# One 1/rms per token tile for the keys of eight heads, and the factor of the query parts moved into the squares

## The chip, the core and the metric

The kernel runs on one core of a Trainium2 chip. The core has engines that each work through their own queue in order: TensorE (PE in the profile, with its weight loads as PEld) for matrix products, VectorE (DVE), ScalarE (ACT) and GpSimd (POOL) for work on elements, SyncE (SP) for starting transfers. Results of TensorE land in a small memory, PSUM, from which ACT or DVE copy them. The metric is the device time of one execution in microseconds; the lower the better.

## The reference

One step of a two-layer streaming encoder. 576 tokens are worked: 512 of a prompt and 64 of a sample that has 512 tokens of past in caches. Every layer adds to x the output projection of three mixers, which share one input projection (stick-breaking attention, gated linear attention, latent attention), then a cross attention into 256 memory tokens, then a gated feed-forward part. The change touches the latent attention alone:

```python
def rmsnorm(x, g):
    y = xf * lax.rsqrt(jnp.mean(xf * xf, axis=-1, keepdims=True) + NORM_EPS)
    return (y * g).astype(x.dtype)

q = (rmsnorm(cq, w['g_cq']) @ w['w_uq']).reshape(B, T, 8, 64 + 32)
q_nope = rmsnorm(q[..., :64], w['g_qn'])
q_rope = rope(rmsnorm(q[..., 64:], w['g_qr']), q_pos)
kv = (lat_all @ w['w_ukv']).reshape(B, L, 8, 64 + 64)
k_nope = rmsnorm(kv[..., :64], w['g_kn'])
v = kv[..., 64:]
s = (q_nope . k_nope + q_rope . k_rope) * 96 ** -0.5        # then a softmax over the visible keys, times v
```

So each head's query has a part of 64 columns and one of 32, each with its own root mean square (rms), and each head's key has 64 columns with one. The keys' rms is taken per token and head.

## The kernel before, in words

Tokens lie in tiles of 128 rows, the last one of 64 (the sample). Products that need near-f32 precision are made of three matmuls: an operand is split into a rounded high part H and a rest L (`copyA` to H on ACT, a subtraction to L on DVE; for weights these are the tiles `wH` and `wL`), and H·H, H·L and L·H are added in PSUM (`mm3`). PSUM has eight banks with three tags: D three, S two, T three.

The order of the work is planned while the program is built. The class `Order` holds the mixers as generators that yield where a result has to come back from another engine, and takes at each step the task of lowest rank that is ready by the class `Clock`, which books each instruction on its engine with an estimated cost. Output-projection products (phase `wout`) and input products have a rank of 10: they fill PE while a task of rank 0 waits. Each engine's queue then has one fixed order, and an instruction waits there for its semaphores, with all that stands behind it.

The two functions of the change:

- `mlaq_units.unit` (lines 1185 to 1218), ten units per layer: two halves `a` of four heads, five token tiles `t`. Six matmuls into an S bank; ACT copies it to `j` (`q3`) and squares it into `u` (`sq`); DVE multiplies the 32-column parts by the gain, POOL by the sine table; DVE sums the squares of both parts of four heads into the eight columns of `s`, line 1208 halves the first four (a mean over 64 from a scaling by 1/32), and `rstd_near` makes 1/rms of all eight at once. POOL multiplies both parts by it (lines 1212 and 1213), PE transposes the four heads into a T bank, ACT copies that into `qT`. The transposes wait for POOL.
- `kv_tile` (lines 1388 to 1415), nine tiles per layer: four of the prompt, four of the past, one of the sample. In a loop over two halves of four heads: three matmuls into an S bank, POOL copies the rotary key in, ACT copies the key part into `j` (`k`), squares it into `kp` (`sq`), copies the values; DVE sums the squares into four columns, `rstd_near` makes 1/rms of the four, DVE multiplies the keys. After the loop PE transposes both halves.

`rstd_near` (lines 386 to 396) is six instructions whatever the width: a tensor_scalar on DVE, Ln and Exp on ACT, and one Newton step of a product and two scalar_tensor_tensor on DVE, in the tiles `s` and `y`. All these lines call helpers, so the profile shows one line, L195, for all of them; instructions are told apart by the tiles' names. `mlaq0` is the phase of the queries in layer 0, `mlak0` that of the keys, `mlap0` the attention of the prompt, `wout0` the output projection, `sb0` the stick-breaking attention.

Of the kernel before, what the change touches and what calls it, by code (L numbers as in the profile page):

```python
# [13 lines left out]
AF = mybir.ActivationFunctionType  # L14
ALU = mybir.AluOpType
AX = mybir.AxisListType
# [162 lines left out]
def behind(tc, ins, earlier):  # L179
    tc.add_manual_dep(ins, earlier.name, mybir.DependencyInfo(mybir.DependencyClass.NoSync, mybir.DependencyReason.DATA),  # L180
                      reason="order of an engine")
# [35 lines left out]
def tile_hybrid(ctx, tc, ins, outs):  # L217
    clock = tc.clock = Clock()
    nc = Engines(tc)
# [16 lines left out]
    def nm(s):  # L236
        uid[0] += 1
        return f"{phase[0]}.{s}_{uid[0]}"
# [26 lines left out]
    def small(n, tag="s"):  # L265
        bufs = {"s": 8, "y": 4}.get(tag, 1)
        return clock.tile(sp.tile([128, 16 if tag == "y" else 8], F32, tag=tag, name=nm(tag), bufs=bufs), tag, bufs)[:, :n]
# [15 lines left out]
    def act(out, in_, func, **kw):  # L283
        name = TABLES.get(func)
        if name is not None and name != held["set"]:
            load = nc.scalar.preload_act_table_set(name).ins
            for i in held["users"]:
                behind(tc, load, i)
            held.update(set=name, load=load, users=[load])
        ins = nc.scalar.activation(out, in_, func, **kw).ins  # L290
        if name is not None:
            behind(tc, ins, held["load"])
            held["users"].append(ins)
# [7 lines left out]
    def tt(out, a, b, op, eng=None):  # L301
        (eng or nc.vector).tensor_tensor(out, a, b, op=op)
# [4 lines left out]
    MUL, ADD, SUB = ALU.mult, ALU.add, ALU.subtract  # L307
# [78 lines left out]
    def rstd_near(ss, inv_n):  # L386

        rows, n = ss.shape[0], ss.shape[1]
        y = small(2 * n, "y")[0:rows]
        y0, z = y[:, 0:n], y[:, n:2 * n]  # L390
        nc.vector.tensor_scalar(ss, ss, inv_n, EPS, op0=MUL, op1=ADD)
        act(z, ss, AF.Ln)
        act(y0, z, AF.Exp, scale=-0.5)
        tt(z, y0, y0, MUL)
        stt(z, z, -0.5, ss, MUL, MUL)
        stt(ss, z, 1.5, y0, ADD, MUL)
# [501 lines left out]
    def layer(l, xn):  # L898
# [283 lines left out]
        def mlaq_units():  # L1182
            hold = {}

            def unit(a, t, r0, rn):
                if a not in hold:
                    hold[a] = load_w(I["w_uq"][l, :, a * 384:(a + 1) * 384], 2, 384, by="k")
                w, cT = hold[a], st["cT"]
                d = ps_("S")[0:rn, 0:384]
                for k in range(2):  # L1190
                    mm3(d, cT[:, k, r0:r0 + rn], cT[:, 2 + k, r0:r0 + rn], w[0](k, 0, 384), w[1](k, 0, 384), k == 0, k == 1)
                if a and t == 4:
                    od.event("mlaqw")
                s = small(8)[0:rn]
                q3 = u("j")[0:rn, 0:384]
                copyA(q3, d)
                sq = u()[0:rn, 0:384]
                act(sq, q3, AF.Square)
                s3, q3 = (x.rearrange("p (h c) -> p h c", c=96) for x in (sq, q3))
                qf = q3[:, :, 64:96]  # L1200
                tt(qf, qf, gbl[0:rn, 160:192].unsqueeze(1).broadcast_to([rn, 4, 32]), MUL)
                qs = small4()[0:rn].rearrange("p (h c) -> p h c", c=32)
                q4, qs4 = (x.rearrange("p h (b c) -> p h b c", c=16) for x in (qf, qs))
                tt(qs4, q4[:, :, ::-1, :], rS[0:rn, t, :].rearrange("p (b c) -> p b c", c=16).unsqueeze(1).broadcast_to(
                    [rn, 4, 2, 16]), MUL, nc.gpsimd)
                nc.vector.tensor_reduce(s[:, 0:4], s3[:, :, 0:64], axis=AX.X, op=ADD)
                nc.vector.tensor_reduce(s[:, 4:8], s3[:, :, 64:96], axis=AX.X, op=ADD)
                nc.vector.tensor_scalar(s[:, 0:4], s[:, 0:4], 0.5, None, op0=MUL)
                tt(q4, q4, rC[0:rn, t, :].unsqueeze(1).unsqueeze(1).broadcast_to([rn, 4, 2, 16]), MUL)
                tt(qf, qf, qs, ADD)  # L1210
                rstd_near(s, 1.0 / 32)
                tt(q3[:, :, 0:64], q3[:, :, 0:64], s[:, 0:4].unsqueeze(2).broadcast_to([rn, 4, 64]), MUL, nc.gpsimd)
                tt(qf, qf, s[:, 4:8].unsqueeze(2).broadcast_to([rn, 4, 32]), MUL, nc.gpsimd)
                yield "T"
                pt = ps_("T").rearrange("p (h c) -> p h c", c=128)
                for h in range(4):
                    tr(pt[0:96, h, 0:rn], q3[:, h, :])
                copyA(qT[a][0:96, :, r0:r0 + rn], pt[0:96, :, 0:rn], scale=gT[0:96, 78 + l:79 + l])

            for a in range(2):  # L1220
                for t, (r0, rn) in enumerate(TILES):
                    yield [f"cT{t}", "sb", "rg"], unit(a, t, r0, rn), None
# [165 lines left out]
        def kv_tile(c0, rn, kr, kT, kc, vdst):  # L1388
            if wkv[0] is None:
                wkv[0] = load_w(I["w_ukv"][l], 1, 1024, by="k")  # L1390
            w, lat = wkv[0], st["lat"]
            ks = []
            vdst = vdst()
            for a in range(2):
                d = ps_("S")[0:rn]
                mm3(d, lat[:, 0, c0:c0 + rn], lat[:, 1, c0:c0 + rn],
                    w[0](0, a * 512, (a + 1) * 512), w[1](0, a * 512, (a + 1) * 512), True, True)
                d3 = d.rearrange("p (h c) -> p h c", c=128)
                k = u("j")[0:rn, 0:384].rearrange("p (h c) -> p h c", c=96)
                sq = u("kp")[0:rn, 0:256].rearrange("p (h c) -> p h c", c=64)  # L1400
                nc.gpsimd.tensor_copy(k[:, :, 64:96], kr().unsqueeze(1).broadcast_to([rn, 4, 32]))
                copyA(k[:, :, 0:64], d3[:, :, 0:64])
                act(sq, k[:, :, 0:64], AF.Square)
                copyA(vdst[a].rearrange("p (h c) -> p h c", c=64), d3[:, :, 64:128])
                q = small(4)[0:rn]
                nc.vector.tensor_reduce(q, sq, axis=AX.X, op=ADD)
                rstd_near(q, 1.0 / 64)
                tt(k[:, :, 0:64], k[:, :, 0:64], q.unsqueeze(2).broadcast_to([rn, 4, 64]), MUL)
                ks.append(k)
            yield "T"  # L1410
            for a in range(2):
                pt = ps_("T").rearrange("p (h c) -> p h c", c=128)
                for h in range(4):
                    tr(pt[0:96, h, 0:rn], ks[a][:, h, :])
                copyA(kT()[a][0:96, :, kc:kc + rn], pt[0:96, :, 0:rn])
# [357 lines left out]
```

## Time and profile before

| what | before |
|---|---|
| median of three timed runs | 1716.88 us (1714.28 to 1719.4) |
| the profiled execution | 1715.26 us |
| its span, first to last instruction | 1713.5 us |
| PE busy | 1649.6 us (96%) |
| DVE busy | 1230.8 us (72%) |
| ACT busy | 903.9 us (53%) |
| POOL busy | 206.8 us (12%) |
| mean granted TensorE clock | 0.99 |

The profile is of one execution; the busy times are shares of its span. Matmuls overlap in TensorE, so two neighbours' durations may cover the same time. Layer 0 runs to some 850 us, layer 1 after it. The queries of the latent attention are made between about 215 and 254 us in layer 0, the key tiles between 249 and 306 us, and the same work of layer 1 lies some 845 us later. Where a wait is told, the engine stood still and the named instruction of the other engine was the last that it waited for.

### The profile page before, as it was taken

Reading aid. Unit: us, or ns where it says so; the run is one execution under the profiler, and the core shown is the slowest. Engines: PE = TensorE matmul, PEld = TensorE weight load, DVE = VectorE, ACT = ScalarE, POOL = GpSimd, SP = SyncE. Lnnn points to the kernel's source line nnn. Section 1 sums busy time; section 2 is a strip of 40 time slices with the busy share of each in tenths; the row PEclk is TensorE's granted clock in tenths of the full one; section 3 lists DMA queues with packets and bytes.
Section 4 is the critical chain, followed back from the end, with each engine's and each line's share of the span. In section 5 each row is a group of like instructions: output and inputs, shape, how many; then the busy total and the mean of one; then the engine's idle time right before and its main releaser. Section 6 shows DMA issues by size and latency. Waiting matters only on the chain.

```text
span 1713.5 us, 30864 instructions
## 1 busy us (share of the span) xinstructions
PE 1649.6 (96%) x12231; PEld 1532.3 (89%) x12231; DVE 1230.8 (72%) x2496; ACT 903.9 (53%) x1929; POOL 206.8 (12%) x303
## 2 busy tenths in 40 slices
PE   8999999999899999999999989999998999999998
PEld 7887887789889999999998978877897999999998
DVE  5737798776898677766657378987669986766763
ACT  6426688655654444344343456886666544334431
POOL 4323341020000000000134042400200000000000
PEclk9999999999999999999998999999999999999999
DMA  5321130022022322222222213200211233233221
GB/s 165 112 72 58 64 116 26 26 74 75 25 80 93 99 80 93 99 85 89 79 83 84 81 47 98 82 26 25 99 50 50 75 99 99 74 99 99 77 97 56
DMA packets 113647, 133.30 MB, mean 78 GB/s; under 512 B 10610, under 2 KB 95712, under 8 KB 113504
## 3 DMA queue, kind: packets, MB, share of 16 engines
q1 hardware_dynamic: 113120, 131.30, 24.2%
q8 instruction: 96, 1.57, 0.4%
q14 instruction: 47, 0.39, 0.1%
q0 software_dynamic: 352, 0.03, 0.0%
q10 hardware_dynamic: 32, 0.01, 0.0%
HBM read 123.64 MB, written 7.68 MB: 77 GB/s over the span
## 4 chain that ended last, share of the span: by engine, by line
PE 76%; DVE 13%; ACT 4%; issue 3%; POOL 2%; DMA 0%; POOLq 0%; ACTq 0%; DVEq 0%
PE ffn1.D L195 9%; PE ffn0.D L195 9%; PE ffn1.S L195 6%; PE ffn1.T L195 6%; PE ffn0.S L195 6%; PE ffn0.T L195 6%; PE win1.D L195 5%; PE win0.D L195 4%; PE cross0.D L195 3%; PE cross1.D L195 3%; PE wout1.D L195 2%; PE wout0.D L195 2%; PE cross0.T L195 1%; PE cross1.T L195 1%; PE mlap1.T L195 1%
## 5 line engine op out<-in xcount | busy, mean ns | idle before, releaser
L195 ACT ACTIVATE ffn1.wH<-ffn1.wraw 128x1024 fp32r<-128x1024 f32 x66 | 60.6, 918 | 115.8 <-PE ffn1.T L195 61.5
L195 ACT ACTIVATE ffn0.wH<-ffn0.wraw 128x1024 fp32r<-128x1024 f32 x66 | 60.6, 918 | 110.5 <-PE ffn0.T L195 60.0
L195 DVE TENSOR_TENSOR ffn1.sL<-ffn1.sum,ffn1.sH 128x1024 fp32r<-128x1024 f32 x44 | 53.7, 1221 | 40.3 <-ACT ffn1.sH L195 40.3
L195 DVE TENSOR_TENSOR ffn0.sL<-ffn0.sum,ffn0.sH 128x1024 fp32r<-128x1024 f32 x44 | 53.7, 1221 | 39.9 <-ACT ffn0.sH L195 39.8
L195 PE MATMUL ffn0.D<-cross0.bT,ffn0.sH 128*128 128x288 f32 x352 | 72.4, 297 | 2.4 <-ACT ffn0.sH L195 1.5
L195 PE MATMUL ffn1.D<-cross1.bT,ffn1.sH 128*128 128x288 f32 x352 | 73.1, 299 | 1.5 <-ACT ffn1.sH L195 0.9
L195 DVE TENSOR_TENSOR ffn0.wL<-ffn0.wraw,ffn0.wH 128x1024 fp32r<-128x1024 f32 x66 | 68.8, 1043 | 7.8 <-ACT ffn0.wH L195 7.2
L195 DVE TENSOR_TENSOR ffn1.wL<-ffn1.wraw,ffn1.wH 128x1024 fp32r<-128x1024 f32 x66 | 68.8, 1043 | 7.8 <-ACT ffn1.wH L195 7.3
L195 PE MATMUL ffn1.S<-cross1.bT,ffn1.sH 128*128 128x288 f32 x352 | 72.6, 297 | 1.0 <-ACT cross1.bT L195 0.5
L195 PE MATMUL ffn0.S<-cross0.bT,ffn0.sH 128*128 128x288 f32 x352 | 71.9, 294 | 0.8 <-ACT cross0.bT L195 0.5
L195 POOL TENSOR_TENSOR ffn0.u<-ffn0.u,ffn0.u 128x576 f32<-128x576 f32 x6 | 10.0, 1664 | 469.5 <-DVE ffn0.wL L195 462.5
L195 ACT ACTIVATE ffn1.sH<-ffn1.sum 128x1024 fp32r<-128x1024 f32 x44 | 46.3, 1055 | 27.1 <-PE ffn1.S L195 22.9
L195 PEld LDWEIGHTS ffn0.D<-cross0.bT,ffn0.sH 128*128 128x128 f32 x352 | 56.7, 189 | 4.0 <-ACT ffn0.sH L195 1.9
L195 ACT ACTIVATE ffn0.sH<-ffn0.sum 128x1024 fp32r<-128x1024 f32 x44 | 46.3, 1055 | 26.0 <-PE ffn0.S L195 22.8
L195 PEld LDWEIGHTS ffn1.D<-cross1.bT,ffn1.sH 128*128 128x128 f32 x352 | 57.3, 191 | 2.9 <-ACT ffn1.sH L195 1.3
L195 PEld LDWEIGHTS ffn1.S<-cross1.bT,ffn1.sH 128*128 128x128 f32 x352 | 57.6, 191 | 1.7 <-ACT cross1.bT L195 0.8
L195 PEld LDWEIGHTS ffn0.S<-cross0.bT,ffn0.sH 128*128 128x128 f32 x352 | 57.0, 189 | 1.4 <-ACT cross0.bT L195 0.8
L195 PE MATMUL ffn1.D<-cross1.bT,ffn1.sL 128*128 128x288 f32 x176 | 52.6, 299 | 0.0
L195 PE MATMUL ffn1.S<-cross1.bT,ffn1.sL 128*128 128x288 f32 x176 | 52.5, 299 | 0.0
L195 PE MATMUL ffn0.D<-cross0.bT,ffn0.sL 128*128 128x288 f32 x176 | 52.4, 298 | 0.0
L195 PE MATMUL ffn0.S<-cross0.bT,ffn0.sL 128*128 128x288 f32 x176 | 52.2, 297 | 0.0
L195 ACT ACTIVATE ffn0.part<-ffn0.D 128x288 f32<-128x288 f32 x66 | 26.9, 408 | 41.7 <-PE ffn0.D L195 41.7
(875 smaller groups left out, 6458.6 us busy)
## 6 DMA issues: line engine op xcount, KB each, us to landing
ffn0.wraw<-in_w_gate_dram SPq DMA_DIRECT2D x11, 1024.0 KB, 5.3
ffn0.wraw<-in_w_up_dram SPq DMA_DIRECT2D x11, 1024.0 KB, 5.5
ffn0.wraw<-in_w_down_dram SPq DMA_DIRECT2D x11, 1024.0 KB, 5.0
ffn1.wraw<-in_w_gate_dram SPq DMA_DIRECT2D x11, 1024.0 KB, 5.3
ffn1.wraw<-in_w_up_dram SPq DMA_DIRECT2D x11, 1024.0 KB, 5.4
ffn1.wraw<-in_w_down_dram SPq DMA_DIRECT2D x11, 1024.0 KB, 5.0
win1.wraw<-in_w_in_dram SPq DMA_DIRECT2D x7, 1024.0 KB, 5.3
win0.wraw<-in_w_in_dram SPq DMA_DIRECT2D x6, 1024.0 KB, 5.7
```

What stands on the lines that cost most here:

```text
L195: r = fn(*args, **kw)
```

## The change

In `kv_tile` the sums of squares of both halves go into one tile of eight columns, `rstd_near` runs once for it after the loop, and the two multiplications of the keys stand behind it. In `mlaq_units.unit` the square is made by two activations, one for the 64-column parts with an input scale of 0.5 ** 0.5 and one for the 32-column parts; the halving of the four sums goes.

```diff
@@ mlaq_units.unit
                 sq = u()[0:rn, 0:384]
-                act(sq, q3, AF.Square)
                 s3, q3 = (x.rearrange("p (h c) -> p h c", c=96) for x in (sq, q3))
+                act(s3[:, :, 0:64], q3[:, :, 0:64], AF.Square, scale=0.5 ** 0.5)
+                act(s3[:, :, 64:96], q3[:, :, 64:96], AF.Square)
...
                 nc.vector.tensor_reduce(s[:, 0:4], s3[:, :, 0:64], axis=AX.X, op=ADD)
                 nc.vector.tensor_reduce(s[:, 4:8], s3[:, :, 64:96], axis=AX.X, op=ADD)
-                nc.vector.tensor_scalar(s[:, 0:4], s[:, 0:4], 0.5, None, op0=MUL)
@@ kv_tile
             vdst = vdst()
+            ss = small(8)[0:rn]
             for a in range(2):
...
                 copyA(vdst[a].rearrange("p (h c) -> p h c", c=64), d3[:, :, 64:128])
-                q = small(4)[0:rn]
-                nc.vector.tensor_reduce(q, sq, axis=AX.X, op=ADD)
-                rstd_near(q, 1.0 / 64)
-                tt(k[:, :, 0:64], k[:, :, 0:64], q.unsqueeze(2).broadcast_to([rn, 4, 64]), MUL)
+                nc.vector.tensor_reduce(ss[:, 4 * a:4 * a + 4], sq, axis=AX.X, op=ADD)
                 ks.append(k)
+            rstd_near(ss, 1.0 / 64)
+            for a, k in enumerate(ks):
+                tt(k[:, :, 0:64], k[:, :, 0:64], ss[:, 4 * a:4 * a + 4].unsqueeze(2).broadcast_to([rn, 4, 64]), MUL)
             yield "T"
```

Since the planner books the instructions as they are made, the order changes on PE, DVE, ACT and POOL through both layers' mixer stages; SP's queue keeps its order, and so do all engines in the other stages. Three places follow.

The first is PE in layer 0, behind the two sums of the stick-breaking norm (`sb0.T`), where the first query unit's product (`j_2523`) is to be transposed. Before, the output projection comes next:

```order
L195 MATMUL mlaq0.S_2606<-mlaq0.wH_2511,win0.cT_1821 128x384
L195 MATMUL sb0.T_2636<-sb0.u_2573,bd_111 128x288
L195 MATMUL sb0.T_2639<-sb0.u_2573,bd_111 128x288
L195 MATMUL wout0.D_2656<-wout0.wH_2648,wout0.mH_1505 128x256
L195 MATMUL wout0.D_2656<-wout0.wL_2649,wout0.mH_1505 128x256
```

After, the transpose and the next unit's product come first:

```order
L195 MATMUL mlaq0.S_2606<-mlaq0.wH_2511,win0.cT_1821 128x384
L195 MATMUL sb0.T_2636<-sb0.u_2573,bd_111 128x288
L195 MATMUL sb0.T_2639<-sb0.u_2573,bd_111 128x288
L195 MATMUL mlaq0.T_2646<-ident,mlaq0.j_2523 96x128 x4
L195 MATMUL mlaq0.S_2652<-mlaq0.wH_2511,win0.cT_1821 128x384
```

The 24 matmuls of that output block stood ahead of the transpose and now stand behind it and behind the six of the next unit.

The second is DVE at the same place: the Newton step of the first unit (`y_2535`, `s_2522`) and the two weight splits of the output projection. Before:

```order
L195 COPY wout0.mkv_2195<-wout0.D_2579 128x256
L195 TENSOR_TENSOR mlaq0.y_2535<-mlaq0.y_2535 128x8
L195 TENSOR_TENSOR wout0.wL_2649<-wout0.wraw_2646,wout0.wH_2648 128x1024
L195 SCALAR_TENSOR_TENSOR mlaq0.y_2535<-mlaq0.y_2535,mlaq0.s_2522 128x8
L195 TENSOR_TENSOR mlaq0.y_2564<-mlaq0.y_2564 128x8
L195 TENSOR_TENSOR wout0.wL_2653<-wout0.wraw_2646,wout0.wH_2652 128x1024
L195 SCALAR_TENSOR_TENSOR mlaq0.s_2522<-mlaq0.y_2535 128x8
```

After:

```order
L195 TENSOR_TENSOR mlaq0.y_2535<-mlaq0.y_2535 128x8
L195 TENSOR_TENSOR mlaq0.j_2552<-mlaq0.j_2552,rC 128x4x32
L195 SCALAR_TENSOR_TENSOR mlaq0.y_2535<-mlaq0.y_2535,mlaq0.s_2522 128x8
L195 TENSOR_SCALAR mlaq0.s_2551<-mlaq0.s_2551 128x8
L195 TENSOR_TENSOR mlaq0.j_2552<-mlaq0.j_2552,mlaq0.s_378_2558 128x4x32
L195 SCALAR_TENSOR_TENSOR mlaq0.s_2522<-mlaq0.y_2535 128x8
L195 COPY wout0.mkv_2195<-wout0.D_2579 128x256
L195 TENSOR_TENSOR wout0.wL_2684<-wout0.wraw_2681,wout0.wH_2683 128x1024
```

Both scalar_tensor_tensor of the first unit have moved ahead of both weight splits; small instructions of the second unit (`j_2552`, `s_2551`) stand between them instead.

The third is DVE at the first key tile of layer 0. Before, each half has its own series (`s_3072`, `y_3074` for the first, `s_3092`, `y_3094` for the second):

```order
L195 TENSOR_REDUCE mlak0.s_3092<-mlak0.kp_3087 128x4
L195 TENSOR_SCALAR mlak0.s_3092<-mlak0.s_3092 128x4
L195 TENSOR_TENSOR mlak0.y_3074<-mlak0.y_3074 128x4
L195 SCALAR_TENSOR_TENSOR mlak0.y_3074<-mlak0.y_3074,mlak0.s_3072 128x4
L195 SCALAR_TENSOR_TENSOR mlak0.s_3072<-mlak0.y_3074 128x4
L195 TENSOR_TENSOR X<-X,wout0.D_3142 128x288
L195 TENSOR_TENSOR mlak0.j_3066<-mlak0.j_3066,mlak0.s_3072 128x4x64
L195 TENSOR_TENSOR mlak0.y_3094<-mlak0.y_3094 128x4
```

After:

```order
L195 TENSOR_REDUCE mlak0.s_3018<-mlak0.kp_3024 128x4
L195 TENSOR_REDUCE mlak0.s_3018<-mlak0.kp_3035 128x4
L195 TENSOR_SCALAR mlak0.s_3018<-mlak0.s_3018 128x8
L195 TENSOR_REDUCE mlak0.s_3050<-mlak0.kp_3056 128x4
L195 TENSOR_TENSOR mlak0.y_3041<-mlak0.y_3041 128x8
L195 SCALAR_TENSOR_TENSOR mlak0.y_3041<-mlak0.y_3041,mlak0.s_3018 128x8
L195 SCALAR_TENSOR_TENSOR mlak0.s_3018<-mlak0.y_3041 128x8
L195 TENSOR_TENSOR mlak0.j_3023<-mlak0.j_3023,mlak0.s_3018 128x4x64
L195 TENSOR_TENSOR mlak0.j_3034<-mlak0.j_3034,mlak0.s_3018 128x4x64
```

One series of eight columns has taken the place of two of four, and the multiplications of both halves (`j_3023`, `j_3034`) follow one another.

## Rows read from the trace of the kernel before

**Rows 1.** The page: busy time by engine, and the chain's shares by engine.
```profile
PE 1649.6 (96%) x12231; PEld 1532.3 (89%) x12231; DVE 1230.8 (72%) x2496; ACT 903.9 (53%) x1929; POOL 206.8 (12%) x303
...
PE 76%; DVE 13%; ACT 4%; issue 3%; POOL 2%; DMA 0%; POOLq 0%; ACTq 0%; DVEq 0%
```

**Rows 2.** Windows: length, busy PE, PEld, DVE, ACT, POOL, clock, DMA.
```profile
225.00:260.00 35.00, 31.01 (x204) 26.77 (x203) 32.61 (x126) 28.13 (x79) 16.17 (x31) 1.00 0.32 109
...
260.00:300.00 40.00, 39.77 (x275) 32.11 (x273) 33.33 (x131) 33.91 (x124) 3.78 (x11) 1.00 0.09 27
...
300.00:340.00 40.00, 39.95 (x273) 27.31 (x272) 31.87 (x87) 27.41 (x66) 0.00 (x0) 1.00 0.09 27
...
1070.00:1105.00 35.00, 31.01 (x205) 26.77 (x204) 32.60 (x124) 27.94 (x78) 16.36 (x32) 1.00 0.32 111
...
245.00:260.00 15.00, 13.94 (x89) 11.65 (x89) 13.77 (x53) 12.82 (x42) 5.64 (x13) 1.00 0.22 71
```

**Rows 3.** Waits of PE, 215 to 265 and 1060 to 1110: total, times, longest.
```profile
PE mlaq0.T L195 <- POOL mlaq0.j L195: 3.6, 6, 1.5
PE mlak0.T L195 <- DVE mlak0.y L195: 0.3, 1, 0.3
...
PE mlaq1.T L195 <- POOL mlaq1.j L195: 3.6, 6, 1.5
```

**Rows 4.** The chain that ended last, 214 to 262: start, us, what.
```profile
218.78 0.60 DVE mlaq0.s L195 x3
...
220.31 1.14 DVE wout0.wL L195
221.60 1.14 DVE wout0.wL L195
...
238.65 1.13 DVE mlaq0.s L195 x4
```

**Rows 5.** Instructions by tile, layer 0: ns min/median/max, first and last start, forms.
```profile
L195 DVE TENSOR_SCALAR mlaq0.s<-mlaq0.s x20: 148/160/603, 218.0 to 248.8; 128x4 f32<-128x4 f32 x8, 128x8 f32<-128x8 f32 x8, 64x4 f32<-64x4 f32 x2, 64x8 f32<-64x8 f32 x2
...
L195 ACT ACTIVATE mlaq0.u<-mlaq0.j x10: 507/520/527, 216.0 to 246.3; 128x384 f32<-128x384 f32 x8, 64x384 f32<-64x384 f32 x2
...
L195 ACT ACTIVATE mlak0.kp<-mlak0.j x18: 399/412/435, 250.9 to 300.5; 128x256 f32<-128x256 f32 x16, 64x256 f32<-64x256 f32 x2
...
L195 DVE TENSOR_SCALAR mlak0.s<-mlak0.s x18: 151/170/414, 252.0 to 301.4; 128x4 f32<-128x4 f32 x16, 64x4 f32<-64x4 f32 x2
...
L195 ACT ACTIVATE mlak0.y<-mlak0.y x18: 187/198/220, 252.7 to 302.7; 128x4 f32<-128x4 f32 x16, 64x4 f32<-64x4 f32 x2
...
L195 DVE SCALAR_TENSOR_TENSOR mlak0.y<-mlak0.y,mlak0.s x18: 144/156/249, 253.2 to 303.2; 128x4 f32<-128x4 f32 x16, 64x4 f32<-64x4 f32 x2
```

**Rows 6.** DVE in order of time: start us, us, operation, tiles.
```profile
217.96 0.16 DVE L195 TENSOR_SCALAR mlaq0.s<-mlaq0.s 128x4 f32<-128x4 f32 x1
218.03 0.28 DVE L195 TENSOR_TENSOR mlaq0.j<-mlaq0.j,rC 128x128 f32<-128x128 f32 x1
...
220.15 0.16 DVE L195 TENSOR_TENSOR mlaq0.y<-mlaq0.y 128x8 f32<-128x8 f32 x1
...
239.18 0.60 DVE L195 TENSOR_SCALAR mlaq0.s<-mlaq0.s 128x4 f32<-128x4 f32 x1
239.70 0.28 DVE L195 TENSOR_TENSOR mlaq0.j<-mlaq0.j,rC 128x128 f32<-128x128 f32 x1
```

**Rows 7.** ACT in order of time: the squares of the first key tile.
```profile
250.87 0.41 ACT L195 ACTIVATE mlak0.kp<-mlak0.j 128x256 f32<-128x256 f32 x1
...
251.70 0.41 ACT L195 ACTIVATE mlak0.kp<-mlak0.j 128x256 f32<-128x256 f32 x1
```

**Rows 8.** PE and POOL in order of time; in brackets the idle time before.
```profile
221.15 0.49 PE L195 MATMUL wout0.D<-wout0.wH,wout0.mH 128*128 128x256 f32 x1
...
228.95 0.64 PE L195 MATMUL mlaq0.T<-ident,mlaq0.j 128*96 128x128 f32 x4 [1.46 <-POOL mlaq0.j L195]
...
222.89 1.05 POOL L195 TENSOR_TENSOR mlaq0.j<-mlaq0.j,mlaq0.s 128x256 f32<-128x256 f32 x2 [3.77 <-DVE mlaq0.y L195]
```

## The prediction

> **What bounds the kernel now.** I read the page first, then the windows around the two places that the change touches, then who waits for whom, the chain of waits, and last the instructions in order of time. The page [rows 1] shows TensorE (PE) busy in 1649.6 of 1713.5 us and the chain that ended last at 76% on PE and 13% on VectorE (DVE): whatever moves the time has to close PE's gaps, 63.9 us in all, since no matmul is added or removed. Most gaps lie elsewhere: the windows of layer 0 [rows 2] show 3.99 us of idle PE between 225 and 260 us, where the queries of the latent attention are made, but only 0.23 us in the next 40 us and 0.05 us in the 40 after that, where most of the key tiles are worked. Layer 1 repeats this to a hundredth of a microsecond (31.01 of 35.00). The waits [rows 3] name the gaps: 3.6 us per layer, in six pieces, is a query transpose that waits for its POOL multiplication, and 0.3 us, once, a key transpose that waits for DVE.
>
> Behind POOL stands DVE. In 225 to 260 DVE is busy 32.61 of 35.00 us, ScalarE (ACT) 28.13, POOL 16.17 [rows 2], and there the chain leaves PE and runs over DVE [rows 4]: sums and scalings of `mlaq0.s`, between them the 1.1 us splits of weights (`wL`). So in this stretch an instruction less on DVE counts; from 260 us on PE is full and it does not.
>
> **The change part by part.** Durations are those of one execution of 1715.26 us (span 1713.5, 1.8 around it); the median of the three timed runs is 1716.88, 1.6 more.
>
> *Queries, the halving on DVE goes.* Ten 4-column tensor_scalar a layer. The row of the stage gives them 0.15 to 0.60 us each with their 8-column sisters [rows 5]; on a full engine what counts is from start to start: 217.96 to 218.03, 0.07, where nothing disturbs, and 239.18 to 239.70, 0.52, where POOL multiplies at the same time [rows 6]. Read so, the ten take 0.07, 0.07, 0.35, 0.28, 0.06, 0.06, 0.52, 0.07, 0.16 and 0.15, together 1.79 us; undisturbed 0.7. Bounds 0.7 to 1.8 us a layer; I take 1.2, since a disturbance can fall on the next instruction instead. The Trainium skill ("VectorE: DVE Perf Modes", section "The DRAIN you can't avoid") says that a DVE operation does not start before the one ahead has emptied the pipe, so that each costs its full duration. By that the undisturbed instruction would give 0.16 us and not 0.07; the trace disagrees, the successor starts 0.09 us before the end [rows 6].
>
> *Queries, one square becomes two.* Ten ACT instructions a layer more. A square of 384 columns takes 0.52 us, one of 256 columns 0.41 [rows 5]; one of 128 the trace does not have, the nearest are 0.20 us (4 columns) and 0.41 (256). So each unit is worth 0.1 to 0.3 us more on ACT, 1 to 3 us a layer, 0 on the path while ACT has its 6.9 idle of 35 us. The first sum can begin some 0.1 us sooner (after 0.41 instead of 0.52) and the second that much later. The chain touches this square once at its start, so I charge 0.3 us a layer, bounds -0.5 to 2.
>
> *Keys, one factor for eight heads.* Each of nine tiles a layer loses one of two series of tensor_scalar, Ln, Exp, product and two scalar_tensor_tensor: 36 DVE and 18 ACT instructions a layer, of 0.16 to 0.17 and 0.20 us [rows 5]. Summed as durations that is 36 x 0.16 = 5.8 us of DVE and 18 x 0.20 = 3.6 us of ACT per layer, the largest term on paper. Hardly any is on the path: of nine tiles two or three fall before 262 us, and PE's idle from 245 to 260 us, where the last query transposes and one key transpose wait, is 1.06 us [rows 2, 3]. I take 0.5 us a layer, bounds 0 to 1.1. The other tiles are hidden by PE: 0.28 us of gaps between 260 and 340 [rows 2].
>
> *Keys, a wait is added.* Heads 0 to 3 now wait for the sums of heads 4 to 7. In before the squares of the two halves of the first tile start 0.83 us apart, 250.87 and 251.70 [rows 7], so a first transpose may come 0.8 us later. Behind it in PE's order stand matmuls of the output projection, which would wait with it. The new order places both transposes of a tile together after other products, and both multiplications next to each other on DVE. With two PSUM banks for these products nothing new is held, because copies, squares and value copies still free the bank first. I cost it at nothing before 262 us; where a filler is missing it is up to 0.8 us a tile.
>
> *The order moves.* It is planned from estimated costs, so a shorter stage comes out in another order: one query transpose goes ahead of 24 output matmuls. In before, POOL was done with its operand at 222.89 + 1.05 = 223.94, while PE began the output matmuls at 221.15 [rows 8]; placed so early it would have waited 2.8 us. But DVE moves with it: both scalar_tensor_tensor of the first unit now come before the two weight splits, which in before stand between them (220.31 and 221.60, 1.14 us each [rows 4]). From the product at 220.15 [rows 6], two more of 0.08 us put POOL's start near 220.4 and its end near 221.45: no wait. Followed on by hand with these durations, the third transpose, which in before started at 228.95 after a wait of 1.46 us [rows 8], starts near 227.8, while a later one (the first of j_2660) waits 0.7 us that it did not. So the order gives and takes; I put it at 0 net, bounds -1.2 to 1.5 a layer.
>
> Sum per layer: -1.2 + 0.3 - 0.5 + 0 = -1.4 us, for two layers -2.8. Against the profiled 1715.26 that is 1712.5; against the median 1716.88 it is 1714.1. I say 1714.0. No query and key term can give more than what PE idles there, 3.99 + 0.28 a layer, 8.5 us in all.
>
> **Rivals.** (a) *Hidden.* The chain on DVE gets shorter, but POOL, 16.17 us with waits on either side, and the new order eat it, as the 0.7 us above would: 1716.9, no change. For it: PE's 96%; that the greater part of what is removed falls where PE is full. Against: DVE, not POOL, is full in 225 to 260.
> (b) *More than the gaps.* PE's busy time hides slack. In 225 to 260 PE is busy 31.01 us but its weight loads only 26.77 [rows 2]; the difference to the window is 8.2 us a layer, 16.5 in both. If the shorter chain frees half of it, the time is 1716.9 - 8.2 = 1708.7. The Trainium skill ("Perfetto Trace Analysis", section "Identifying the Most-Contended Engine") holds matmul busy time a bad measure because matmuls are pipelined, and takes the share of weight loads instead, which is this reading. Against it here: in 300 to 340, where PE has no gap, weight loads are at 27.31 of 40, so a good part of that difference belongs to the kind of matmul.
> (c) *Slower.* Transposes stand ahead of filler that used to cover the wait, and POOL is not done. Where one stalls PE, the 24 matmuls behind it stall too. Price: 2.8 us at the first place if the factor comes when it did in before, 0.7 at the second, in both layers 7.0: 1723.9. It decides if POOL ends j_2523 later than some 222.7 us instead of 221.45, half of the way. For it: in before PE waits six times for just this operand. Against: the two weight splits have visibly left the chain.
>
> **How the numbers follow.** Forecast (a gain of 1 to 5 us) 0.50, its own range 1711.5 to 1716; (a) 0.18; (b) 0.23; (c) 0.09. 0.3% is 5.2 us, so faster means below 1711.7: most of (b), 0.19, and the upper edge of the forecast, 0.08, make 0.27. Slower means above 1722: most of (c), 0.07, and 0.01 from (a). The rest is 0.65. The three runs of before lie from 1714.28 to 1719.4, which adds some 2 us to either side. The range 1709 to 1719 takes in the forecast, (a) and the nearer half of (b).
>
> **What would show it.** Right: PE's idle in the query stretch falls from 4.0 to between 2 and 3 us in each layer, the waits of the query transposes from 3.6 to 2 or 3 us, the next 80 us stay without gaps; DVE's busy time drops by 7 to 14 us over the kernel (92 instructions of 0.07 to 0.16 us) and hardly any of it is seen in the span. The first query transpose after the stick-breaking sums waits less than 0.5 us. Wrong: new PE waits for key transposes or for scores between 260 and 340 us (then the joined factor came too late), a first query transpose that waits over 1 us (rival c), or a span that loses more than PE's idle does (rival b).

## The result, and the profile after

The changed kernel takes 1732.45 us, median of four runs (1730.23 to 1734.72); the kernel before, on the same chip, 1716.12 (1714.28 to 1719.40). The ratio is 1.0087, with a 95% interval of 1.0070 to 1.0104: slower by some 15 us (12 to 18), by the medians 16.3. The forecast was 1714.0, in a range of 1709 to 1719. It was wrong in its sign.

The busy line of the changed kernel's page, against the first lines of [rows 1]:

```profile
PE 1657.2 (96%) x12231; PEld 1535.1 (89%) x12231; DVE 1227.6 (71%) x2404; ACT 901.9 (52%) x1913; POOL 207.5 (12%) x303
```

VectorE (DVE) has 92 instructions fewer, as it should, but only 3.2 us less of busy time. TensorE (PE) has the same 12231 matmuls and is busy 7.6 us longer. The windows that answer to [rows 2]; columns are the stretch, its length, and busy time (with instructions) of PE, PEld, DVE, ACT and POOL, the granted TensorE clock, DMA share and GB/s:

```profile
225.00:260.00 35.00, 27.90 (x187) 24.42 (x187) 29.53 (x95) 23.30 (x66) 17.47 (x31) 1.00 0.33 106
260.00:300.00 40.00, 39.97 (x279) 32.39 (x278) 31.97 (x108) 31.95 (x111) 3.03 (x10) 1.00 0.11 36
300.00:340.00 40.00, 39.74 (x248) 26.31 (x247) 31.02 (x93) 28.50 (x78) 1.16 (x4) 1.00 0.08 27
1070.00:1105.00 35.00, 28.47 (x196) 25.55 (x195) 30.36 (x97) 26.41 (x71) 16.28 (x28) 1.00 0.33 103
```

In the query stretch PE's idle time has grown from 3.99 to 7.10 us in layer 0 and to 6.53 us in layer 1. DVE, which was full there, now idles too, 5.5 us instead of 2.4. From 260 to 340 us there is as little idle as before. The waits that answer to [rows 3]:

```profile
PE mlaq0.T L195 <- POOL mlaq0.j L195: 7.3, 6, 1.8
PE mlaq1.T L195 <- POOL mlaq1.j L195: 6.9, 6, 1.8
```

Twice 3.6 us has become 7.3 and 6.9. The fixed windows mislead a little, since the changed kernel is late in them, so I cut the stretch by events. The *query stage* goes from the first query product on PE to the start of the last query transpose, the *rest* from there to the last product of the output projection. First the kernel before, then the changed one, layer 0:

```profile
213.96:253.44 39.48, 35.84 (x242) 32.28 (x240) 36.14 (x129) 31.76 (x78) 17.83 (x33) 1.00 0.40 128
253.44:378.61 125.17, 122.92 (x901) 96.95 (x902) 100.47 (x305) 89.56 (x269) 13.75 (x20) 1.00 0.12 38
```

```profile
216.84:257.72 40.88, 33.20 (x224) 29.53 (x222) 34.49 (x109) 28.75 (x77) 19.34 (x33) 1.00 0.31 99
257.72:388.00 130.28, 128.32 (x920) 100.47 (x920) 100.13 (x278) 91.56 (x263) 13.10 (x20) 1.00 0.13 44
```

Both stretches together are 6.51 us longer, 171.16 instead of 164.65; in layer 1 it is 5.16 (1069.10 to 1238.90 against 1059.16 to 1223.80). With the 2.9 us by which the first query product is late, this is 14.6 of the 15.0 us between the two spans. Those 2.9 us come ahead of any changed instruction and are scatter between executions: PE's queue is the same up to there in all runs below but the two with a dearer POOL, and in the traces read here the first query product starts anywhere from 214 to 217.6 us (queries_old_order, whose time equals that of the kernel before, starts at 216.98). So the traces place 11.7 us of the loss in the two mixer stages, just under the 12 that the interval begins with; where more than that is lost, no trace here shows it.

How the 6.51 us come about can be read off the four rows. The query stage is 1.40 us longer although it holds 18 matmuls fewer (x224 for x242); counted in PE's queue these are 12 output products and 6 key products that the new order places behind the stage. The rest is 5.11 us longer: it holds 19 matmuls more (one lies across a border of the cut), 2.6 us at the 0.136 us each of before (122.92 / 901), and its matmuls take 0.139 us on the mean (128.32 / 920), 2.8 us in all, with 0.3 us less idle. Added up over both stretches, PE idles 9.6 us instead of 5.9, the 3.7 us by which the named waits grew, and is busy 2.8 us longer on the same 1142 matmuls; in layer 1 the two parts are 2.9 and 2.2 us. Why the query stage itself is longer, although DVE has less to do in it, no run settles.

The query transposes of the changed kernel on PE (start, duration, instruction, and in brackets the wait ahead of it), against the first wait in [rows 8]:

```profile
225.76 0.64 PE L195 MATMUL mlaq0.T<-ident,mlaq0.j 128*96 128x128 f32 x4 [1.35 <-POOL mlaq0.j L195]
232.58 0.64 PE L195 MATMUL mlaq0.T<-ident,mlaq0.j 128*96 128x128 f32 x4 [0.78 <-POOL mlaq0.j L195]
235.60 0.42 PE L195 MATMUL mlaq0.T<-ident,mlaq0.j 128*96 128x128 f32 x2 [1.80 <-POOL mlaq0.j L195]
244.99 0.64 PE L195 MATMUL mlaq0.T<-ident,mlaq0.j 128*96 128x128 f32 x4 [1.10 <-POOL mlaq0.j L195]
248.82 0.64 PE L195 MATMUL mlaq0.T<-ident,mlaq0.j 128*96 128x128 f32 x4 [1.62 <-POOL mlaq0.j L195]
254.49 0.64 PE L195 MATMUL mlaq0.T<-ident,mlaq0.j 128*96 128x128 f32 x4 [0.70 <-POOL mlaq0.j L195]
```

The first one, which was to wait less than 0.5 us, waits 1.35. What POOL and DVE did then: POOL's two multiplications of that unit together and the second of them by itself, then DVE's Newton step that releases them and the weight split behind it:

```profile
223.75 1.95 POOL L195 TENSOR_TENSOR mlaq0.j<-mlaq0.j,mlaq0.s 128x256 f32<-128x256 f32 x2 [0.83 <-DVE mlaq0.s L195]
...
224.32 1.38 POOL L195 TENSOR_TENSOR mlaq0.j<-mlaq0.j,mlaq0.s 128x128 f32<-128x128 f32 x1
```

```profile
223.51 0.16 DVE L195 SCALAR_TENSOR_TENSOR mlaq0.s<-mlaq0.y 128x8 f32<-128x8 f32 x1
223.59 0.42 DVE L195 COPY wout0.mkv<-wout0.D 128x256 f32<-128x256 f32 x1
223.93 1.52 DVE L195 TENSOR_TENSOR wout0.wL<-wout0.wraw,wout0.wH 128x1024 fp32r<-128x1024 f32 x1
...
225.65 1.21 DVE L195 TENSOR_TENSOR wout0.wL<-wout0.wraw,wout0.wH 128x1024 fp32r<-128x1024 f32 x1
```

Set back by the 2.88 us of the later start, POOL began at 220.87 (foreseen: 220.4) and ended at 222.82 (foreseen: 221.45). The pair takes 1.95 us here and 1.05 in [rows 8], so that 0.90 of the 1.37 us by which POOL ended late are its own, and 0.47 come from the series ahead of it.

### The profile page after: what moved, and what is told of

Read it like the earlier page. It is cut to its first block, busy times and chain, and to the rows that moved or that the text cites. A ratio compares the mean times of both kernels' runs of the same rounds, so it can differ in the third digit from the quotient of the medians.

```text
span 1728.5 us, 30747 instructions
## 1 busy us (share of the span) xinstructions
PE 1657.2 (96%) x12231; PEld 1535.1 (89%) x12231; DVE 1227.6 (71%) x2404; ACT 901.9 (52%) x1913; POOL 207.5 (12%) x303
## 4 chain that ended last, share of the span: by engine, by line
PE 77%; DVE 10%; ACT 4%; POOL 3%; issue 3%; DMA 1%; POOLq 0%; ACTq 0%; DVEq 0%; SPq 0%
PE ffn0.D L195 9%; PE ffn1.D L195 8%; PE ffn1.S L195 6%; PE ffn0.S L195 6%; PE ffn0.T L195 6%; PE ffn1.T L195 6%; PE win1.D L195 4%; PE win0.D L195 4%; PE cross0.D L195 3%; PE cross1.D L195 3%; PE wout1.D L195 3%; PE wout0.D L195 2%; PE mlap1.T L195 1%; PE mlap0.T L195 1%; PE cross1.T L195 1%
```

## The experiments

There were two ideas at the start. **Theory A:** the new order of the queues costs. **Theory B:** the changed instructions cost (keys that come late, the second square). To part them I held orders fixed: the queue of every engine in the mixer stages of one kernel was recorded and put on the instructions of another by ordering dependencies that carry no semaphore, with the planner's choices replayed:

```diff
+            SEEN.setdefault(self.key, []).append(r.ins)
...
+    for e, text in ORDER.items():
...
+        for i, j in zip(seq, seq[1:]):
+            behind(tc, SEEN[e][j], SEEN[e][i])
```

PE's and POOL's queues are then the recorded ones row for row. The runs, with layer 0 cut as above (us, and PE's matmuls in it; keys_only is told below); before stands for 1715.96 to 1716.88, the medians of the kernel before beside each run:

| run | instructions | order | median us | ratio to before, 95% interval | query stage | rest |
|---|---|---|---|---|---|---|
| before | old | old | 1716 | 1 | 39.48 (242) | 125.17 (901) |
| after | new | new | 1732.45 | 1.0087, 1.0070 to 1.0104 | 40.88 (224) | 130.28 (920) |
| new_ops_old_order | new | old | 1739.05 | 1.0128, 1.0113 to 1.0144 | 39.36 (242) | 135.75 (902) |
| old_ops_new_order | old | new | 1739.97 | 1.0135, 1.0122 to 1.0149 | 44.49 (223) | 132.46 (920) |
| queries_only | new queries | planned anew | 1728.92 | 1.0074, 1.0062 to 1.0087 | 42.17 (224) | 129.30 (920) |
| queries_old_order | new queries | old | 1718.29 | 1.0001, 0.9990 to 1.0012 | 39.37 (242) | 125.52 (901) |
| no_halving | old, 10 a layer less | old | 1715.88 | 0.9999, 0.9990 to 1.0008 | 39.24 (243) | 125.08 (902) |
| keys_only_again | new keys | planned anew | 1721.20 | 1.0023, 1.0013 to 1.0033 | 39.97 (241) | 127.03 (902) |
| old_ops_keys_order | old | of keys_only | 1723.49 | 1.0038, 1.0026 to 1.0050 | 39.49 (241) | 128.43 (901) |
| old_pool_dearer | old | planned anew | 1726.58 | 1.0055, 1.0042 to 1.0069 | 43.52 (258) | 132.68 (941) |
| new_pool_dearer | new | planned anew | 1734.21 | 1.0096, 1.0080 to 1.0113 | 45.18 (258) | 134.31 (941) |
| new_order_mul_on_dve | new, POOL's on DVE | new | 1729.82 | 1.0071, 1.0054 to 1.0088 | 41.75 (227) | 130.11 (919) |
| new_filler_first | new | new but PE | 1727.97 | 1.0072, 1.0058 to 1.0086 | 40.91 (224) | 130.37 (919) |
| old_filler_first | old | old but PE | 1716.87 | 1.0004, 0.9993 to 1.0016 | 39.97 (245) | 124.70 (899) |
| new_no_rotary | new, less | new | 1721.40 | 1.0026, 1.0015 to 1.0038 | 36.57 (223) | 130.49 (921) |
| old_no_rotary | old, less | old | 1712.77 | 0.9980, 0.9970 to 0.9990 | 37.58 (241) | 125.65 (901) |

(In the two rows with a dearer POOL the first query product stands elsewhere in the queue, so their stages compare with each other only.)

The granted TensorE clock has to be read beside the stages. It is 1.00 in the query stage of all but four of these traces, and 0.96 in those of queries_only, old_ops_new_order, new_filler_first and new_order_mul_on_dve (of the last in layer 0 alone). At 0.96 PE is busy for 34.7 to 35.0 us with nearly the same matmuls that take it 33.2 in the changed kernel. In the rest it is 0.99 for new_ops_old_order and old_pool_dearer.

**Instructions and order exchanged.**

> All instructions of the changed kernel, none of the old ones, but every engine's queue held in the order that the kernel before has (PE and POOL row for row; on DVE and ACT the removed rows are missing, the second square stands beside the first, and the key multiplication of heads 0 to 3 directly ahead of that of heads 4 to 7). Theory A, the new order is what costs: the loss goes, 1711 to 1718 us against 1716 of the kernel before, and the query transposes wait at most 3.6 us a layer. Theory B, the changed instructions cost (the joined factor's later keys, the extra square on ScalarE): the loss stays, 1726 to 1734 us, with new waits for mlak transposes between 250 and 310 us.

> All instructions of the kernel before, but every engine's queue held in the order that the changed kernel has (PE and POOL row for row; on DVE and ACT the rows that the change removed stand beside their counterparts). Theory A, the order costs: about as slow as the changed kernel or a little slower, 1730 to 1738 us, and the query transposes wait some 7 us a layer for POOL. Theory B, the instructions cost: 1714 to 1720 us.

Both crosses are slower than either kernel; neither theory had that for the first, and the second lies a little above theory A's 1730 to 1738. Waits of PE in new_ops_old_order:

```profile
PE mlak0.T L195 <- DVE mlak0.j L195: 9.1, 8, 2.1
PE mlaq0.T L195 <- POOL mlaq0.j L195: 3.5, 5, 1.4
```

The query waits are those of before, 3.5 us for 3.6. Nearly all that is lost stands in the keys: in the old order a transpose of heads 0 to 3 comes early, and now it needs the sums of heads 4 to 7. This is the wait that the change adds, and PE waits 9.1 us a layer for it where the order does not give way. In the changed kernel, whose order puts both transposes later, it is gone. In old_ops_new_order it is the queries that PE waits for, more than in the changed kernel:

```profile
PE mlaq0.T L195 <- POOL mlaq0.j L195: 9.2, 8, 2.0
```

Its query stage is 3.6 us longer than that of the changed kernel; half of this is idle, the other half busy time at the lower clock. So theory A holds for the queries: the new order makes PE wait with either set of query instructions (9.2 and 7.3 us), the old one serves both (3.6 and 3.5). For the keys it is the new instructions in the old order that do not fit.

**The two parts apart.**

> The query part of the change alone (two squares, no halving), keys as before; its order on PE and POOL is that of the changed kernel up to the end of the query transposes and a third one behind. Theory A: the query waits are those of the changed kernel, some 7 us a layer against 3.6, so 6 to 9 us are lost there in the two layers, and the rest depends on the order behind: 1722 to 1732 us. Theory B with the joined keys as its cause: 1714 to 1719 us; with the extra square as its cause: 1728 to 1734.

> The key part of the change alone (one factor for eight heads), queries as before; its order is that of the kernel before up to the end of the query transposes and another one behind. Theory A: query waits as in the kernel before, 3.6 us a layer, the order behind may give or take 2 to 3 us a layer: 1714 to 1722 us. Theory B with the joined keys as its cause: 1726 to 1734 us, and PE waits for mlak transposes.

The edits are the two halves of the diff of the change. queries_only came out at 1728.92, keys_only at 1720.90 (ratio 1.0020, 1.0008 to 1.0032): 12.5 and 4.5 us over before, together 17.0, about the 16.3 of the whole. The queries take most of it; their waits are those of the changed kernel:

```profile
PE mlaq0.T L195 <- POOL mlaq0.j L195: 7.1, 6, 1.8
```

Behind some of these waits the granted clock fell in this run, by the same columns as above:

```profile
230.00:235.00 5.00, 2.43 (x17) 1.70 (x15) 4.39 (x11) 3.29 (x8) 3.61 (x5) 1.00 0.22 81
235.00:240.00 5.00, 5.00 (x24) 4.89 (x25) 1.55 (x9) 1.77 (x6) 0.45 (x1) 0.66 0.36 105
...
245.00:250.00 5.00, 2.44 (x15) 1.96 (x16) 4.99 (x16) 2.43 (x9) 3.32 (x5) 1.00 0.15 34
250.00:255.00 5.00, 4.73 (x34) 4.19 (x32) 4.42 (x19) 3.29 (x8) 3.03 (x8) 1.00 0.52 205
```

PE had been busy 2.43 of 5 us; in the next 5 the clock is 0.66 on the mean, so for a good part of them at the lower of its two levels (1.2 instead of 2.4 GHz), and PE gets through 24 matmuls with no idle. The second pair of rows is as sparse ahead, 2.44 of 5 us, and there the clock stayed at 1.00, so such a row alone does not tell when it falls. PE's busy time in the stage is 1.5 us longer than in the changed kernel, whose clock stayed at 1.00, and its idle time 0.2 us less; that is the whole difference between 42.17 us of stage here and 40.88 there.

For a trace of the keys alone the kernel was run once more:

> The key part of the change alone, once more, for a trace: its time was 0.2% above the kernel before. If the joined factor delays key transposes, PE waits for mlak tiles, 1 to 2 us a layer; if not, the query waits are at most 3.6 us and what is lost lies in the attention stage without a named wait. 1718 to 1722 us.

```profile
PE mlaq0.T L195 <- POOL mlaq0.j L195: 3.7, 6, 1.5
PE mlak0.T L195 <- DVE mlak0.j L195: 0.2, 1, 0.2
```

The queries are as before and the keys wait 0.2 us; the rest is 1.9 us longer than before, without a named wait. Its 902 matmuls take 125.10 us there instead of 122.92 for 901.

**What the query instructions are worth at an unchanged order.**

> The query part of the change alone (two squares, no halving), keys as before, every engine's queue held in the order of the kernel before. It measures what the changed query instructions are worth by themselves. The prediction's two terms (1.2 us gained, 0.3 us lost a layer) would give 1714.5 us against 1716.4. If the removed halvings free nothing on the path, as the unchanged 3.5 us of query waits in the held run of the whole change suggest, 1715.5 to 1718. If the second square costs, 1720 or more.

The diff is the query part of the change, held. 1.0001 of before: nothing won, nothing lost. The waits hardly move:

```profile
PE mlaq0.T L195 <- POOL mlaq0.j L195: 3.5, 5, 1.4
```

> The kernel before in its own order without the ten halvings a layer on VectorE, and with nothing in their place: the factor 0.5 is left out of the computation, so that the removal alone is measured, without the second square on ScalarE. The prediction's term (1.2 us a layer) gives 1714.0 against 1716.4. If the removed instructions free nothing at the end of the series, 1716 to 1717.

```diff
-                nc.vector.tensor_scalar(s[:, 0:4], s[:, 0:4], 0.5, None, op0=MUL)
```

0.9999 of before (0.9990 to 1.0008, so at most 1.7 us for both layers). Even without the second square the ten halvings give nothing that can be measured. DVE's busy time in the query stage falls by 0.83 us (36.14 to 35.31 in the windows of the stage), the stage by 0.24.

**Is it the planner's belief in an early POOL?**

> The changed kernel with one number of the planner changed: it books a POOL tensor_tensor at 0.0045 us an element instead of 0.0021, so the transposes are planned later and in all another order comes out, with 23 to 27 output matmuls together ahead of a transpose twice in the query stage. If the order alone makes the loss (theory A) and the planner's belief in an early POOL is its cause, the query waits fall to 4 us or less a layer and the time to 1715 to 1724 us. If not, it stays at 1730 or goes up.

> The kernel before with the same one number of the planner changed, no instruction added or removed. Its order differs from that of the kernel before in as many places as that of the changed kernel does. If the order is what moves the time (theory A), it differs from 1716.4 us by more than 3 us on either side, 1708 to 1728; if the order hardly matters, 1715 to 1718.

```diff
-        return 0.15 + n * (0.0021 if op == "tensor_tensor" else 0.0035)
+        return 0.15 + n * (0.0045 if op == "tensor_tensor" else 0.0035)
```

No for the first: waits of 5.1 us a layer, 1734 us. For the second, the kernel before without a single instruction changed, one number of the planner costs 10 us. That is the plainest proof of theory A's premise: the order by itself moves this kernel by 0.55%, more than half of what the change did.

**What in the new order costs?** Theory C took POOL, theory D the series ahead of it:

> The changed kernel in its own order on every engine, but the two multiplications of the queries by 1/rms on VectorE, directly behind the Newton step that gives the factor, instead of on POOL. Theory C, what the early transposes wait for is POOL, whose multiplications take up to 1.95 us beside a weight split on VectorE: the six waits of 7.3 us a layer fall under 3.5 us and the time to 1722 to 1727 us against 1732 of the changed kernel. Theory D, the series ahead of the multiplications is late itself (its Ln, Exp and Newton step behind other work): the transposes wait 5 us or more a layer, now for VectorE, and the time is 1730 to 1737 us, since VectorE gets some 6 us a layer more.

```diff
-                tt(q3[:, :, 0:64], q3[:, :, 0:64], s[:, 0:4].unsqueeze(2).broadcast_to([rn, 4, 64]), MUL, nc.gpsimd)
-                tt(qf, qf, s[:, 4:8].unsqueeze(2).broadcast_to([rn, 4, 32]), MUL, nc.gpsimd)
+                tt(q3[:, :, 0:64], q3[:, :, 0:64], s[:, 0:4].unsqueeze(2).broadcast_to([rn, 4, 64]), MUL)
+                tt(qf, qf, s[:, 4:8].unsqueeze(2).broadcast_to([rn, 4, 32]), MUL)
```

```profile
PE mlaq0.T L195 <- DVE mlaq0.j L195: 6.4, 7, 1.7
```

With POOL off the path the transposes still wait 6.4 us, now for DVE. In layer 0 the stage is no shorter, at a lower clock; in layer 1, where the clock stayed at 1.00, it is 39.7 us for 40.4. So POOL's part is 0.7 us there, and theory C falls as the main cause; the median lies just under D's 1730 to 1737. Next, the transposes that wait were set behind their neighbours in PE's queue, in both kernels:

> The changed kernel, every engine in its own order, but on PE six of the ten query transposes of a layer, those that wait in its trace, stand behind the next 5 to 12 matmuls (products of the next queries, output projection) instead of ahead of them. Nothing else moves. Theory A, these transposes stand too early in PE's queue: the waits fall from 7.3 us a layer to 2 to 4, and the time by 6 to 10 us, to 1722 to 1726. Theory E, the pace of the query stage is set by the series through ScalarE, VectorE and POOL, and PE's work only shifts: the waits reappear at later transposes, 5 us or more, and the time is 1728 to 1733.

> The kernel before, every engine in its own order, but on PE five of the ten query transposes of a layer stand behind the next 2 to 12 output matmuls, which cover the wait that each has in the trace of before. Theory A: of the 3.6 us a layer some 2 to 3 go, 1711 to 1713.5 us against 1716.4, faster than both kernels. Theory E: the waits come back at later transposes, 1715 to 1718.

The first of these places in new_filler_first, in PE's queue (in all, units 1, 3, 4, 6, 7 and 9 of a layer moved there by 6, 5, 6, 5, 12 and 5 rows, and units 3, 4, 6, 8 and 10 in old_filler_first by 12, 4, 6, 2 and 4):

```diff
 MATMUL sb0.T_2639<-sb0.u_2573,bd_111 128x288
-MATMUL mlaq0.T_2646<-ident,mlaq0.j_2523 96x128 x4
 MATMUL mlaq0.S_2652<-mlaq0.wH_2511,win0.cT_1821 128x384
...
 MATMUL mlaq0.S_2652<-mlaq0.wH_2511,win0.cT_1821 128x384
+MATMUL mlaq0.T_2646<-ident,mlaq0.j_2523 96x128 x4
```

PE's waits, first in new_filler_first, then in old_filler_first:

```profile
PE mlaq0.T L195 <- POOL mlaq0.j L195: 4.2, 5, 1.6
PE mlaq0.S L195 <- ACT mlaq0.wH L195: 1.0, 1, 1.0
```

```profile
PE mlaq0.S L195 <- ACT mlaq0.wH L195: 1.7, 1, 1.7
PE mlaq0.T L195 <- POOL mlaq0.j L195: 1.1, 3, 0.7
```

The waits of the transposes fall by 3.1 and by 2.5 us a layer, and the mixer stage stays where it was: 171.28 us for 171.16, and 164.67 for 164.65. In old_filler_first, at a clock of 1.00, this is plain: PE runs ahead and waits elsewhere, for the second half of the query weights (`mlaq0.wH`, 1.7 us). In new_filler_first the clock also falls, as above:

```profile
230.00:235.00 5.00, 3.70 (x18) 3.23 (x16) 3.23 (x11) 3.03 (x8) 2.14 (x3) 0.75 0.40 109
```

Its stage therefore belongs beside that of queries_only, whose query instructions and their order are those of the changed kernel and whose clock is the same. First queries_only, then new_filler_first:

```profile
216.50:258.67 42.17, 34.71 (x224) 30.97 (x222) 34.37 (x109) 28.64 (x77) 19.41 (x33) 0.96 0.30 94
214.12:255.03 40.91, 35.02 (x224) 31.25 (x222) 34.36 (x109) 28.77 (x77) 18.92 (x33) 0.96 0.31 96
```

At the same clock the stage is 1.3 us shorter (1.4 in layer 1) where the waits of the transposes are some 3 us less. So in the old order a wait that the profile names at a transpose was not the price of that transpose's place, and in the new order it was so for less than half. In old_filler_first theory A's gain of 3 to 5 us did not come; 1716.87 is what theory E expected. In new_filler_first the median, 1727.97, lies just under E's 1728 to 1733 and 4.5 us under that of the changed kernel; the intervals of the two ratios overlap, but a gain of a few us is not excluded. What was left as the main idea is theory E, a pace set by the elementwise series of the queries:

> The changed kernel in its own order on every engine, with the rotation of the queries' 32-column parts left out of the computation (two VectorE and one POOL instruction less a unit, twenty and ten a layer). PE's queue is the same row for row. If the pace of the query stage is set by the elementwise series (theory E), the waits of the query transposes fall from 7.3 to under 4 us a layer, the stage from its first product to its last transpose from 40.9 to under 38.5 us, and the time to 1722 to 1727 us against 1732. If PE is late for another reason (weight splits, banks), waits and time stay within 1 us a layer: 1729 to 1733.

> The same piece left out of the kernel before, in its own order. Theory E: waits from 3.6 to under 2 us a layer, the stage from 39.5 to under 38, the time 1711 to 1714 us. Otherwise 1715 to 1717.

```diff
-                tt(qs4, q4[:, :, ::-1, :], rS[0:rn, t, :].rearrange("p (b c) -> p b c", c=16).unsqueeze(1).broadcast_to(
-                    [rn, 4, 2, 16]), MUL, nc.gpsimd)
...
-                tt(q4, q4, rC[0:rn, t, :].unsqueeze(1).unsqueeze(1).broadcast_to([rn, 4, 2, 16]), MUL)
-                tt(qf, qf, qs, ADD)
```

The windows of the two stretches in new_no_rotary, and its waits:

```profile
217.33:253.90 36.57, 32.56 (x223) 29.50 (x221) 27.76 (x89) 28.36 (x77) 14.15 (x23) 1.00 0.34 110
253.90:384.39 130.49, 128.48 (x921) 100.49 (x920) 100.21 (x278) 91.71 (x263) 13.12 (x20) 1.00 0.13 44
```

```profile
PE mlaq0.T L195 <- POOL mlaq0.j L195: 3.9, 5, 1.6
```

At the same PE queue and a clock of 1.00 the stage shrinks by 4.3 us and the waits by 3.4, the rest does not move, and 1721.40 us is a little below what was expected. In the kernel before the stage shrinks by 1.9 us and the waits to 2.2 (expected: under 2). So both runs go theory E's way, in the new order more than in the old: the series through ScalarE, DVE and POOL set how long the query stage lasts, and PE's idle in it is that length less the work which the order puts there. The rotation takes work from DVE and from POOL, so which of the engines sets it is not told apart. The new order puts 18 matmuls less into the stage. That this lack is what PE's longer idle consists of is arithmetic from the rows; moving them back was not tried.

**The keys: order or joined factor?**

> All instructions of the kernel before, every engine held in the order of the kernel that has the key part of the change alone (1721, 0.23% above before, no named wait). If the order of the attention stage costs (theory A), 1719 to 1724 us, with PE's 1142 matmuls of the stage taking some 161 us as there, not 158.8 as before. If the joined factor costs, 1715 to 1718.

1723.49 us, with none of the change's instructions in it:

```profile
257.11:385.54 128.43, 125.93 (x901) 97.06 (x902) 99.26 (x307) 89.12 (x270) 13.16 (x20) 1.00 0.11 37
```

901 matmuls, as many as in before, take 125.93 us instead of 122.92. So it is the order here too; at a given order the joined factor costs nothing more. Why the same matmuls take longer in that order is open: PE idles only 0.25 us more, the clock is 1.00, and PE's queue changes between plain and rounded operands no more often (118 times through the stage, 122 in before).

No version that computes the same beat the kernel before; the new queries in its order equal it.

## Why the prediction was wrong, point by point

- **"The order moves. [...] I put it at 0 net, bounds -1.2 to 1.5 a layer."** This step failed. In layer 0 the new order costs 6.5 us and in layer 1 5.2. I followed single transposes by hand, with durations from an undisturbed stretch, and netted gains and losses at PE's waits. What the runs showed in its place: the new order leaves 18 matmuls less inside the query stage, where PE then idles 4.0 us more, and behind it the same matmuls take 2.8 us longer (layer 0). Neither has a place in that sum. That the order does it is shown by the held runs; why the matmuls behind the stage take longer stays open.
- **The halving, 1.2 us a layer.** Mis-sized: nothing measurable (0.9999), 0.24 us by the stage. DVE is busy for 36.1 of the stage's 39.5 us, but taking 0.83 us off it shortens the stage by less than a third of that. Counting start to start on a full engine gave its busy time, not the stage's. The rotation, 4.4 us of DVE and 4.9 of POOL a layer, gave 1.9 us in the same order. (The section of the Trainium skill that the prediction names there, "The DRAIN you can't avoid" in "VectorE: DVE Perf Modes", goes on to say that a next operation which is not held starts earlier; so the 0.07 us from start to start do not speak against the page.)
- **The second square, 0.3 us a layer.** Nothing to be seen: with it and without it the held runs lie at 1.0001 and 0.9999. So small a term is within their intervals.
- **The joined keys, 0.5 us a layer won, and the added wait, nothing.** The wait is free in the new order as foreseen, with no key wait between 260 and 340 us. But it is free because the order gives way, and that order costs about 2 us a layer; held in the old order PE waits 9.1.
- **Rival (c).** Its point came: POOL was done at 222.82, set back to the start of before, past the 222.7 that it named. Its price, 7.0 us for both layers, is just what the named waits grew by (7.3 + 6.9 against 7.2), but that is luck: it charged 2.8 us to the first place, which waited 1.35, and 0.7 to a second, while six places waited. The two mixer stages grew by 11.7 us, and the runs with the transposes moved show that those waits are in good part a symptom. Its chance of 0.09 was far too low. The Trainium skill ("SBUF — State Buffer", section "Who interferes with whom") says that a DVE operation with both inputs in SBUF and a GpSimd operation that reads SBUF exclude each other, and that the later one stands still. I had not weighed it; the trace agrees: POOL's second multiplication stood from 224.32 to 225.70 and ended 0.25 us after DVE's split (223.93 to 225.45), and the split, begun while POOL's first was at work, took 1.52 us where the next one, alone, took 1.21. It is not new with the change: over both layers POOL's 128-column multiplications that lie for the greater part beside a weight split took 1.40 to 1.65 us in before (four of them) and 1.11 to 1.45 in the changed kernel (five), the others 0.39 to 0.53.
- **Rival (b)** did not occur: PE's busy time went up, not down.
- **What was to show it:** the signs for "wrong" were there, a first transpose that waits over 1 us and an idle that grows from 4.0 to 7.1 us. DVE's busy time fell by 3.2 us, not by the 7 to 14 that were to be seen: other operations became longer, the split of 1.52 us among them.

## What to carry to other kernels

Where a planner sets the queues, an edit is two changes, its instructions and a new order, and the second can be the larger by far: hold the order to price the first. An order that fits its instructions is easily lost: three other orders of the very same instructions cost 0.4 to 1.4% here (old_ops_keys_order, old_pool_dearer, old_ops_new_order). And a wait shown at an instruction is not yet that instruction's price: cut the stage by events, count the matmuls in it, and see what sets its length. Compare stages only at the same granted clock: here a lower one hid a gain of 1.3 us.

## What the runs showed of the hardware

Two POOL multiplications took 1.95 us instead of 1.05 where a 1024-column split ran on DVE, which itself took 1.52 instead of 1.21. After 5 us in which PE was busy for 2.43, the granted clock was 0.66 over the next 5; after another such 5 us of the same trace (2.44 busy) it stayed at 1.00. At a clock of 1.00 some 900 matmuls of one stretch took 122.92 us in one order of PE's queue and 125.93 in another.
